# Two rows of a softmax to a partition: row-pair tiles, and template loads on another queue

## Chip, cores, metric

One Trainium2 chip, one of its cores, nothing else running. The metric is device microseconds (us) of one execution, lower is better; medians are over unprofiled and profiled executions of the same kernel. Profiles are single executions; their span is about 2 us shorter than the time. Profiled runs were fast (granted clock 1.0), and ratios use fast runs alone.

## The reference

A relative position bias is added to attention logits, then a softmax over the last axis:

```python
# logits (2, 8, 2112, 2112) float32, rel_bias (8, 33) float32
rel = clip(pos[:, None] - pos[None, :], -16, 16) + 16
logits = logits + rel_bias[:, rel]
e = exp(logits - logits.max(-1, keepdims=True))
return e / e.sum(-1, keepdims=True)
```

285.5 MB come in and 285.5 MB go out (2 x 8 x 2112 x 2112 x 4 bytes each). Outside a diagonal band 33 columns wide the bias is one constant per head on each side.

## The kernel before

The 33,792 rows of 2112 floats are cut into 264 tiles of 128 rows, one row to a partition. SyncE issues the load of a tile, VectorE (DVE) adds a band from a per-head template, ScalarE (ACT) takes exponentials left and right of the band's end with the constant as its bias and sums them, VectorE scales by the reciprocal, GpSimd (POOL) issues the store. SyncE also loads the templates.

```python
    io = ctx.enter_context(tc.tile_pool(name="io", bufs=20))
    ...
    def load_template(t, p0, np_, h):
        x = const.tile([P, BAND], FP32, tag="X", name="X", bufs=4)
        nc.sync.dma_start(out=x[p0 : p0 + np_], in_=bass.AP(... ap=[[1, np_], [1, BAND]]))
        nc.vector.tensor_copy(out=t[p0 : p0 + np_], in_=bass.AP(... [-1, BAND]))   # reversed
    ...
    for t in range(NT):                                  # 264 tiles
        rs = P * t
        ...
        L = io.tile([P, S], FP32, tag="L")
        nc.sync.dma_start(out=L, in_=logits_f[rs : rs + P, :])
        ...                                              # band add, exps with sums, per head segment
        nc.vector.reciprocal(out=tot, in_=tot)
        nc.vector.tensor_scalar_mul(out=L[:], in0=L[:], scalar1=tot[:])
        nc.gpsimd.dma_start(out=out_f[rs : rs + P, :], in_=L[:])
```

The softmax here doesn't subtract the row's maximum and nothing guards it: scores larger than these inputs give would overflow.

Of the kernel before, what the change touches and what calls it, by code (L numbers as in the profile page):

```python
# [1 line left out]

# [4 lines left out]

FP32 = mybir.dt.float32
EXP = mybir.ActivationFunctionType.Exp  # L10
ADD = mybir.AluOpType.add


@with_exitstack
def kernel(
    ctx: ExitStack,
    tc: tile.TileContext,
    logits: bass.AP,
    rel_bias: bass.AP,
    out: bass.AP,  # L20
):
    nc = tc.nc
    P = 128
    B, H, S, S2 = logits.shape
    assert S == S2
    MR = 16
    W = 2 * MR + 1
    BAND = P + 2 * MR
    EXT = P - 1
    ELEN = 2 * EXT + W  # L30

    logits_f = logits.flatten_outer_dims()
    out_f = out.flatten_outer_dims()
    NR = B * H * S
    assert NR % P == 0
    NT = NR // P

    const = ctx.enter_context(tc.tile_pool(name="const", bufs=1))
    dram = ctx.enter_context(tc.tile_pool(name="dram", bufs=1, space=bass.MemoryType.DRAM))

    rb8 = const.tile([H, W], FP32, tag="rb8")
    nc.sync.dma_start(out=rb8, in_=rel_bias)
    rbB = const.tile([P, H, W], FP32, tag="rbB")
    nc.sync.dma_start(
        out=rbB,
        in_=bass.AP(tensor=rel_bias.tensor, offset=rel_bias.offset, ap=[[0, P], [1, H * W]]),
    )

    e8 = const.tile([H, ELEN], FP32, tag="e8")
    nc.vector.tensor_copy(out=e8[:, 0:EXT], in_=rb8[:, 0:1].to_broadcast([H, EXT]))  # L50
    nc.vector.tensor_copy(out=e8[:, EXT : EXT + W], in_=rb8[:, :])  # L51
    nc.vector.tensor_scalar(  # L52
        out=e8[:, 0 : EXT + W],
        in0=e8[:, 0 : EXT + W],
        scalar1=rb8[:, W - 1 : W],
        scalar2=None,
        op0=mybir.AluOpType.subtract,
    )
    nc.vector.memset(e8[:, EXT + W :], 0.0)  # L59
    eD = dram.tile([H, ELEN], FP32, tag="eD")  # L60
    nc.sync.dma_start(out=eD, in_=e8)

    def load_template(t, p0, np_, h):
        x = const.tile([P, BAND], FP32, tag="X", name="X", bufs=4)
        nc.sync.dma_start(
            out=x[p0 : p0 + np_],
            in_=bass.AP(
                tensor=eD.tensor,
                offset=eD.offset + h * ELEN,
                ap=[[1, np_], [1, BAND]],  # L70
            ),
        )
        nc.vector.tensor_copy(  # L73
            out=t[p0 : p0 + np_],
            in_=bass.AP(
                tensor=x.tensor,
                offset=x.offset + p0 * list(x.ap[0])[0] + (BAND - 1),
                ap=[[list(x.ap[0])[0], np_], [-1, BAND]],
            ),
        )  # L80

    T = []
    for h in range(H):
        t = const.tile([P, BAND], FP32, tag=f"T{h}", name="T")
        load_template(t, 0, P, h)
        T.append(t)
    TP = []
    for k in range(H // 2):
        t = const.tile([P, BAND], FP32, tag=f"TP{k}", name="TP")
        load_template(t, 0, 64, 2 * k)  # L90
        load_template(t, 64, 64, 2 * k + 1)
        TP.append(t)
    io = ctx.enter_context(tc.tile_pool(name="io", bufs=20))
    small = ctx.enter_context(tc.tile_pool(name="small", bufs=16))

    def rb_at(h, k, p0, p1):
        return rbB[p0:p1, h, k : k + 1]

    for t in range(NT):
        rs = P * t  # L100
        f0 = rs // S
        f1 = (rs + P - 1) // S
        if f0 == f1:
            segs = [(0, P, f0, rs - f0 * S)]
        else:
            split = f1 * S - rs
            segs = [(0, split, f0, rs - f0 * S), (split, P, f1, 0)]

        L = io.tile([P, S], FP32, tag="L")
        nc.sync.dma_start(out=L, in_=logits_f[rs : rs + P, :])  # L110

        def seg_ab(p0, p1, i0):
            n = p1 - p0
            c0 = i0 - MR
            return c0, max(c0, 0), min(i0 + n + MR, S)

        max_slots = 1
        for (p0, p1, f, i0) in segs:
            _, _, b = seg_ab(p0, p1, i0)
            max_slots = max(max_slots, 1 + (b < S))  # L120

        s = None
        if max_slots == 2:
            s = small.tile([P, 2], FP32, tag="s", name="s")
        tot = small.tile([P, 1], FP32, tag="tot")

        for (p0, p1, f, i0) in segs:
            h = f % H
            n = p1 - p0
            c0, a, b = seg_ab(p0, p1, i0)  # L130
            nslots = 1 + (b < S)
            if len(segs) == 1:
                tmpl = T[h]
            else:
                tmpl = TP[(f0 % H) // 2]
            nc.vector.tensor_tensor(  # L136
                out=L[p0:p1, a:b],
                in0=L[p0:p1, a:b],
                in1=tmpl[p0 : p0 + n, a - c0 : b - c0],
                op=ADD,  # L140
            )
            acc0 = s[p0:p1, 0:1] if max_slots == 2 else tot[p0:p1, 0:1]
            nc.scalar.activation(  # L143
                out=L[p0:p1, 0:b],
                in_=L[p0:p1, 0:b],
                func=EXP,
                bias=rb_at(h, W - 1, p0, p1),
                accum_out=acc0,
            )
            if nslots == 2:  # L150
                nc.scalar.activation(  # L151
                    out=L[p0:p1, b:S],
                    in_=L[p0:p1, b:S],
                    func=EXP,
                    bias=rb_at(h, 0, p0, p1),
                    accum_out=s[p0:p1, 1:2],
                )
            elif max_slots == 2:
                nc.vector.memset(s[p0:p1, 1:2], 0.0)  # L159

        if max_slots == 2:
            nc.vector.tensor_tensor(out=tot, in0=s[:, 0:1], in1=s[:, 1:2], op=ADD)  # L162
        nc.vector.reciprocal(out=tot, in_=tot)  # L163

        nc.vector.tensor_scalar_mul(out=L[:], in0=L[:], scalar1=tot[:])  # L165

        nc.gpsimd.dma_start(out=out_f[rs : rs + P, :], in_=L[:])  # L167


# [1 line left out]
_INS = ['logits', 'rel_bias']  # L171
_OUTS = [((2, 8, 2112, 2112), 'float32')]


# [23 lines left out]
```

## Time and profile before

| | before |
|---|---|
| time, median | 1363.65 us (4 runs, 1362.85 to 1364.25) |
| span of the profile | 1361.6 us |
| DMA rate, steady part (100 to 1300 us) | 427.5 GB/s |
| bytes moved, all queues | 572.4 MB |
| span less bytes / steady rate | 1361.6 - 1339.1 = 22.5 us |
| ACT, DVE, POOL busy | 48%, 38%, 10% |

Rates to a tenth are summed from the packet records of the trace, between 100 and 1300 us; the views give whole GB/s. A packet is here one record of the profile: one contiguous run that one DMA engine moved. Besides the data there are records of 4 bytes, 9 ns long at the median, 16 to a DMA (8737 for the 547 DMAs of before); I take them for the signal that one of the 16 engines has done its part, and call them completions.

From the profile page of before: span, engine shares, then the span in 40 equal slices (tenths of the 16 DMA engines' busy time, and GB/s in each), the DMA queues with packets, MB and share of the 16 engines, the chain that ended last, and the issues with KB each and the median time to landing.

```profile
span 1361.6 us, 3994 instructions
DVE 518.4 (38%) x1084; ACT 657.6 (48%) x1057; POOL 140.6 (10%) x268
...
DMA  8999999999999999999999999999999999999996
GB/s 296 414 427 428 428 427 428 428 427 427 428 428 427 428 428 427 427 428 428 427 428 428 427 427 428 428 427 428 428 426 427 428 427 427 428 428 426 428 429 287
DMA packets 78030, 572.36 MB, mean 420 GB/s; under 512 B 8744, under 2 KB 10416, under 8 KB 10416
...
q1 hardware_dynamic: 39984, 286.62, 50.4%
q0 software_dynamic: 38016, 285.49, 49.7%
...
DMA 98%; issue 1%; DVE 0%; ACT 0%; SPq 0%; POOLq 0%; POOL 0%; ACTq 0%; DVEq 0%
...
L<-in_logits_dram SPq DMA_DIRECT2D x264, 1056.0 KB, 40.5
out_dram<-L POOLq DMA_DIRECT2D x264, 1056.0 KB, 15.2
```

No compute engine is busy more than half of the span (ACT, the most, 48%), while the two DMA queues together fill 100% of the 16 engines. The rate is flat at 426 to 429 GB/s and sags only in the first two slices and the last. So there are two things to gain: the rate itself, and the two ends. Of the packets, 2 x 33,792 are whole rows of 8448 B.

The beat of the steady part, from the timeline of before (start in us, duration, engine, line, operation):

```profile
305.82 0.53 POOL L167 DMA_DIRECT2D out_dram<-L  x1 [4.53 <-DVE L L165]
310.88 0.53 POOL L167 DMA_DIRECT2D out_dram<-L  x1 [4.52 <-DVE L L165]
315.94 0.53 POOL L167 DMA_DIRECT2D out_dram<-L  x1 [4.53 <-DVE L L165]
```

One tile every 5.06 us: 2,162,688 bytes in and out of it, so 427 GB/s.

What SyncE's queue waited for, from its waits (us in total, times, longest):

```profile
SPq L110 <- DMA L<-in_logits_dram: 1152.9, 252, 4.9
...
SPq L65 <- DMA X<-eD: 10.3, 7, 3.2
```

Each new load waits for an earlier load to land, not for a free buffer: with a landing time of 40.5 us and a beat of 5.06 us, eight loads are in flight at any time, and the 20 buffers are not what holds them. The second line is the start: on the same queue the template loads (L65) waited 10.3 us for their staging buffers, and the logits loads behind them waited too. By 22 us only five had been issued.

The two ends, from the stretch view of before (stretch, length, busy us of DVE, ACT, POOL with instruction counts, clock, DMA share, GB/s):

```profile
0.00:20.00 20.00, 6.22 (x20) 8.56 (x13) 1.41 (x6) 1.00 0.79 229
20.00:40.00 20.00, 7.91 (x21) 5.86 (x9) 1.55 (x3) 1.00 1.00 380
...
100.00:1300.00 1200.00, 460.57 (x952) 587.67 (x945) 125.92 (x237) 1.00 1.01 427
1337.00:1341.00 4.00, 0.95 (x3) 2.42 (x4) 0.53 (x1) 1.00 0.99 410
1341.00:1345.00 4.00, 1.71 (x4) 1.41 (x3) 0.00 (x0) 1.00 0.43 182
1345.00:1349.00 4.00, 2.08 (x5) 1.03 (x3) 1.06 (x2) 1.00 0.63 262
1349.00:1353.00 4.00, 1.48 (x2) 2.12 (x2) 0.03 (x1) 1.00 0.77 319
1353.00:1357.00 4.00, 0.00 (x0) 0.00 (x0) 0.50 (x1) 1.00 0.68 281
```

At the end the DMA engines run below their rate while ACT and DVE still work on the last tiles: nothing else is left to move.

### The profile page before, as it was taken

The numbers are of one execution on the slowest core, as the hardware profiler recorded it, in microseconds if no ns is written. First come the engines' busy times: TensorE is split into PE (matmuls) and PEld (weight loads), VectorE is DVE, ScalarE is ACT, GpSimd is POOL, SyncE is SP. The second block draws the span as 40 slices with busy tenths as digits, with TensorE's granted clock in tenths as the row PEclk, the third lists the DMA queues.
The fourth block names the chain that finished last, engine by engine and source line by source line (L and its number), as shares of the span: only waits on it lengthen the run. The fifth ranks groups of instructions, "written<-read, shape, count | busy, mean of one in ns | idle before, by whom it ended". The sixth has DMA issues, their size and how long they took to land.

```text
span 1361.6 us, 3994 instructions
## 1 busy us (share of the span) xinstructions
DVE 518.4 (38%) x1084; ACT 657.6 (48%) x1057; POOL 140.6 (10%) x268
## 2 busy tenths in 40 slices
DVE  3434343343334333333343333333433433333432
ACT  3454444544445444454444544445444454444543
POOL 0011011010101111011011010101101101101100
DMA  8999999999999999999999999999999999999996
GB/s 296 414 427 428 428 427 428 428 427 427 428 428 427 428 428 427 427 428 428 427 428 428 427 427 428 428 427 428 428 426 427 428 427 427 428 428 426 428 429 287
DMA packets 78030, 572.36 MB, mean 420 GB/s; under 512 B 8744, under 2 KB 10416, under 8 KB 10416
## 3 DMA queue, kind: packets, MB, share of 16 engines
q1 hardware_dynamic: 39984, 286.62, 50.4%
q0 software_dynamic: 38016, 285.49, 49.7%
q14 instruction: 30, 0.25, 0.0%
HBM read 286.59 MB, written 285.48 MB: 420 GB/s over the span
## 4 chain that ended last, share of the span: by engine, by line
DMA 98%; issue 1%; DVE 0%; ACT 0%; SPq 0%; POOLq 0%; POOL 0%; ACTq 0%; DVEq 0%
DMA L<-in_logits_dram 96%; DMA X<-eD 1%; DMA eD<-e 0%; ACT L L143 0%; SPq L110 0%; DMA rb<-in_rel_bias_dram 0%; DVE L L165 0%; DVE T L73 0%; POOLq L193 0%; DVE tot L162 0%; POOL out_dram L167 0%; ACT L L151 0%; DVE tot L163 0%; DVE L L136 0%; DVE e L52 0%
## 5 line engine op out<-in xcount | busy, mean ns | idle before, releaser
L151 ACT ACTIVATE L<-L,rbB 128x1968 f32<-128x1968 f32 (+31 forms) x256 | 297.1, 1160 | 654.0 <-DMA L<-in_logits_dram 651.0
L165 DVE TENSOR_SCALAR L<-L,tot 128x2112 f32<-128x2112 f32 x264 | 348.4, 1320 | 8.4
L143 ACT ACTIVATE L<-L,rbB 128x144 f32<-128x144 f32 (+33 forms) x272 | 333.2, 1225 | 30.5 <-DVE L L136 23.7
L167 POOL DMA_DIRECT2D out_dram<-L x264 | 140.4, 532 | 1212.7 <-DVE L L165 1050.2
L136 DVE TENSOR_TENSOR L<-L,T 128x160 f32<-128x160 f32 (+1 forms) x256 | 82.9, 324 | 350.3 <-DMA L<-in_logits_dram 348.9
L162 DVE TENSOR_TENSOR tot<-s 128x1 f32<-128x1 f32 x256 | 40.6, 159 | 422.9 <-ACT L L143 422.3
L163 DVE RECIPROCAL tot<-tot 128x1 f32<-128x1 f32 x264 | 43.2, 164 | 26.3 <-ACT L L143 17.7
L143 ACT ACTIVATION_READ_ACCUMULATOR L<-L,rbB 128x1 f32 (+1 forms) x272 | 50.7, 186 | 0.0
L151 ACT ACTIVATION_READ_ACCUMULATOR L<-L,rbB 128x1 f32 (+1 forms) x256 | 47.7, 186 | 0.0
L136 DVE TENSOR_TENSOR L<-L,TP 64x80 f32<-64x80 f32 x16 | 3.8, 236 | 7.2 <-DMA L<-in_logits_dram 6.9
L73 DVE COPY T<-X 128x160 f32<-128x160 f32 x8 | 1.7, 240 | 11.9 <-DMA X<-eD 11.9
L151 ACT ACT_TABLE_LOAD x1 | 1.3, 1283 | 9.1 <-DMA L<-in_logits_dram 9.1
L73 DVE COPY TP<-X 64x160 f32<-64x160 f32 x8 | 1.9, 238 | 5.2 <-DMA X<-eD 5.1
L50 DVE COPY e<-rb 8x127 f32<-8x127 f32 x1 | 0.2, 215 | 1.2 <-DMA rb<-in_rel_bias_dram 1.2
L59 DVE MEMSET e<- 8x127 f32 x1 | 0.2, 164 | 0.8 <-PEq L182 0.8
L159 DVE MEMSET s<- 64x1 f32 x8 | 0.5, 59 | 0.0
L52 DVE TENSOR_SCALAR e<-e,rb 8x160 f32<-8x160 f32 x1 | 0.3, 291 | 0.0
L51 DVE COPY e<-rb 8x33 f32<-8x33 f32 x1 | 0.2, 160 | 0.0
L182 POOL MEMSET const-float32-0.0<- 128x1 f32 x1 | 0.1, 98 | 0.2 <-issue 0.2
L182 POOL MEMSET const-bfloat16-1.0<- 128x1 bf16 x1 | 0.1, 102 | 0.0
L182 POOL MEMSET const-float32-1.0<- 128x1 f32 x1 | 0.1, 98 | 0.0
L182 POOL MEMSET const-uint8-127<- 128x1 uint8 x1 | 0.1, 98 | 0.0
## 6 DMA issues: line engine op xcount, KB each, us to landing
L<-in_logits_dram SPq DMA_DIRECT2D x264, 1056.0 KB, 40.5
out_dram<-L POOLq DMA_DIRECT2D x264, 1056.0 KB, 15.2
X<-eD SPq DMA_DIRECT2D x8, 80.0 KB, 4.4
X<-eD SPq DMA_DIRECT2D x8, 40.0 KB, 7.8
rbB<-in_rel_bias_dram SPq DMA_DIRECT2D x1, 132.0 KB, 5.3
rb<-in_rel_bias_dram SPq DMA_DIRECT2D x1, 1.0 KB
eD<-e SPq DMA_DIRECT2D x1, 9.0 KB
```

What stands on the lines that cost most here:

```text
L50: nc.vector.tensor_copy(out=e8[:, 0:EXT], in_=rb8[:, 0:1].to_broadcast([H, EXT]))
L52: nc.vector.tensor_scalar(out=e8[:, 0 : EXT + W], in0=e8[:, 0 : EXT + W], scalar1=rb8[:, W - 1 : W], scalar2=None, op0=mybir.AluOpType.sub ...
L73: nc.vector.tensor_copy(out=t[p0 : p0 + np_], in_=bass.AP(tensor=x.tensor, offset=x.offset + p0 * list(x.ap[0])[0] + (BAND - 1), ap=[[list ...
L136: nc.vector.tensor_tensor(out=L[p0:p1, a:b], in0=L[p0:p1, a:b], in1=tmpl[p0 : p0 + n, a - c0 : b - c0], op=ADD,)
L143: nc.scalar.activation(out=L[p0:p1, 0:b], in_=L[p0:p1, 0:b], func=EXP, bias=rb_at(h, W - 1, p0, p1), accum_out=acc0,)
L151: nc.scalar.activation(out=L[p0:p1, b:S], in_=L[p0:p1, b:S], func=EXP, bias=rb_at(h, 0, p0, p1), accum_out=s[p0:p1, 1:2],)
L159: nc.vector.memset(s[p0:p1, 1:2], 0.0)
L162: nc.vector.tensor_tensor(out=tot, in0=s[:, 0:1], in1=s[:, 1:2], op=ADD)
L163: nc.vector.reciprocal(out=tot, in_=tot)
L165: nc.vector.tensor_scalar_mul(out=L[:], in0=L[:], scalar1=tot[:])
L167: nc.gpsimd.dma_start(out=out_f[rs : rs + P, :], in_=L[:])
L182: nc = _bacc.Bacc("TRN2", target_bir_lowering=False, num_devices=1)
```

## The change

Its intent: make each DMA transfer longer and contiguous. A tile now takes 256 rows, and partition p holds rows 2p and 2p+1, which are neighbours in memory and in the partition: 16,896 contiguous bytes on both sides. Buffers become 9 of two rows. The last 256 rows stay two single tiles. Because a row in the band now moves by two columns per partition, templates are 287 columns wide instead of 160, a segment that starts inside a tile needs its own template, and the template loads move to POOL's queue with two staging buffers.

```diff
+    KB = 2
+    NTAIL = 2
...
     def load_template(...):
-        x = const.tile([P, BAND], FP32, tag="X", name="X", bufs=4)
-        nc.sync.dma_start(
+        x = const.tile([P, width], FP32, tag=f"X{width}", name="X", bufs=2)
+            nc.gpsimd.dma_start(                      # stride KB per partition
...
-    io = ctx.enter_context(tc.tile_pool(name="io", bufs=20))
+    io = ctx.enter_context(tc.tile_pool(name="io", bufs=9))
...
-        L = io.tile([P, S], FP32, tag="L")
-        nc.sync.dma_start(out=L, in_=logits_f[rs : rs + P, :])
+        L = io.tile([P, kb, S], FP32, tag=f"L{kb}", bufs=9 if kb == KB else 2)
+        nc.sync.dma_start(
+            out=L,
+            in_=logits_f[rs : rs + n, :].rearrange("(p j) c -> p j c", j=kb),
+        )
...                                                    # per j: band add, exps, scale
-        nc.gpsimd.dma_start(out=out_f[rs : rs + P, :], in_=L[:])
+        nc.gpsimd.dma_start(
+            out=out_f[rs : rs + n, :].rearrange("(p j) c -> p j c", j=kb),
+            in_=L[:],
+        )
```

More of the change, by code (lines that the diff above doesn't have):

```diff
@@ L27 @@
     W = 2 * MR + 1
-    BAND = P + 2 * MR
-    EXT = P - 1
+    KB = 2
+    NTAIL = 2
+    EXT = KB * (P - 1)
     ELEN = 2 * EXT + W
@@ L34 @@
     NR = B * H * S
-    assert NR % P == 0
-    NT = NR // P
+    assert NR % (KB * P) == 0
+    NBLK = NR // (KB * P) - (NTAIL + KB - 1) // KB
     const = ctx.enter_context(tc.tile_pool(name="const", bufs=1))
@@ L61 @@
     nc.sync.dma_start(out=eD, in_=e8)
-    def load_template(t, p0, np_, h):
-        x = const.tile([P, BAND], FP32, tag="X", name="X", bufs=4)
-        nc.sync.dma_start(
-            out=x[p0 : p0 + np_],
-            in_=bass.AP(
-                tensor=eD.tensor,
-                offset=eD.offset + h * ELEN,
-                ap=[[1, np_], [1, BAND]],
-            ),
-        )
-        nc.vector.tensor_copy(
-            out=t[p0 : p0 + np_],
-            in_=bass.AP(
-                tensor=x.tensor,
-                offset=x.offset + p0 * list(x.ap[0])[0] + (BAND - 1),
-                ap=[[list(x.ap[0])[0], np_], [-1, BAND]],
-            ),
-        )
@@ L82, with legal_split @@
-    T = []
-    for h in range(H):
-        t = const.tile([P, BAND], FP32, tag=f"T{h}", name="T")
-        load_template(t, 0, P, h)
-        T.append(t)
-    TP = []
-    for k in range(H // 2):
-        t = const.tile([P, BAND], FP32, tag=f"TP{k}", name="TP")
-        load_template(t, 0, 64, 2 * k)
-        load_template(t, 64, 64, 2 * k + 1)
-        TP.append(t)
-    io = ctx.enter_context(tc.tile_pool(name="io", bufs=20))
+    def legal_split(p0, p1):
+        return [(p0, min(64, p1)), (64, p1)] if 0 < p0 < 64 < p1 else [(p0, p1)]
@@ new lines, in load_template @@
+    def load_template(t, p0, np_, h, stride, width):
+        off0 = EXT + 2 * MR - (width - 1)
+        assert off0 >= 0 and off0 + stride * (np_ - 1) + width <= ELEN
+        x = const.tile([P, width], FP32, tag=f"X{width}", name="X", bufs=2)
+        xpitch = list(x.ap[0])[0]
+        for (pa, pb) in legal_split(p0, p0 + np_):
+            nc.gpsimd.dma_start(
+                out=x[pa:pb],
+                in_=bass.AP(
+                    tensor=eD.tensor,
+                    offset=eD.offset + h * ELEN + off0 + stride * (pa - p0),
+                    ap=[[stride, pb - pa], [1, width]],
+                ),
+            )
+            nc.vector.tensor_copy(
+                out=t[pa:pb],
+                in_=bass.AP(
+                    tensor=x.tensor,
+                    offset=x.offset + pa * xpitch + (width - 1),
+                    ap=[[xpitch, pb - pa], [-1, width]],
+                ),
+            )
@@ new lines @@
+    W2 = KB * (P - 1) + 2 * MR + 1
+    W1 = (P - 1) + 2 * MR + 1
+    tmpl_req = {}
+    groups = []
+    r = 0
+    while r < NR:
+        kb = KB if r < NBLK * KB * P else 1
+        n = kb * P
+        f0 = r // S
+        f1 = (r + n - 1) // S
+        if f0 == f1:
+            segs = [(0, P, f0, r - f0 * S)]
+        else:
+            sp = (f1 * S - r) // kb
+            assert sp * kb == f1 * S - r and 0 < sp < P
+            segs = [(0, sp, f0, r - f0 * S), (sp, P, f1, 0)]
+        out_segs = []
+        for (p0, p1, f, i0) in segs:
+            h = f % H
+            key = (p0, h, kb)
+            if key not in tmpl_req:
+                tmpl_req[key] = (p0, P - p0, h, kb, W2 if kb == KB else W1)
+            out_segs.append((p0, p1, f, i0, key))
+        groups.append((r, kb, out_segs))
+        r += n
@@ L94 @@
+    assert r == NR
+    TMPL = {}
+    for key, (p0, np_, h, stride, width) in sorted(tmpl_req.items()):
+        t = const.tile([P, width], FP32, tag=f"T{key}", name="T")
+        load_template(t, p0, np_, h, stride, width)
+        TMPL[key] = t
+    io = ctx.enter_context(tc.tile_pool(name="io", bufs=9))
     small = ctx.enter_context(tc.tile_pool(name="small", bufs=16))
@@ L97, in rb_at @@
         return rbB[p0:p1, h, k : k + 1]
-    for t in range(NT):
-        rs = P * t
-        f0 = rs // S
-        f1 = (rs + P - 1) // S
-        if f0 == f1:
-            segs = [(0, P, f0, rs - f0 * S)]
-        else:
-            split = f1 * S - rs
-            segs = [(0, split, f0, rs - f0 * S), (split, P, f1, 0)]
-        L = io.tile([P, S], FP32, tag="L")
-        nc.sync.dma_start(out=L, in_=logits_f[rs : rs + P, :])
-        def seg_ab(p0, p1, i0):
-            n = p1 - p0
-            c0 = i0 - MR
-            return c0, max(c0, 0), min(i0 + n + MR, S)
-        max_slots = 1
-        for (p0, p1, f, i0) in segs:
-            _, _, b = seg_ab(p0, p1, i0)
-            max_slots = max(max_slots, 1 + (b < S))
-        s = None
-        if max_slots == 2:
-            s = small.tile([P, 2], FP32, tag="s", name="s")
-        tot = small.tile([P, 1], FP32, tag="tot")
-        for (p0, p1, f, i0) in segs:
-            h = f % H
-            n = p1 - p0
-            c0, a, b = seg_ab(p0, p1, i0)
-            nslots = 1 + (b < S)
-            if len(segs) == 1:
-                tmpl = T[h]
-            else:
-                tmpl = TP[(f0 % H) // 2]
+    for (rs, kb, segs) in groups:
+        n = kb * P
+        L = io.tile([P, kb, S], FP32, tag=f"L{kb}", bufs=9 if kb == KB else 2)
+        nc.sync.dma_start(
+            out=L,
+            in_=logits_f[rs : rs + n, :].rearrange("(p j) c -> p j c", j=kb),
+        )
+        s = small.tile([P, kb, 2], FP32, tag="s")
+        tot = small.tile([P, kb], FP32, tag="tot")
+        maxslots = [1] * kb
+        info = []
+        for (p0, p1, f, i0, key) in segs:
+            np_ = p1 - p0
+            ww = kb * (np_ - 1) + 2 * MR + 1
+            pranges = legal_split(p0, p1)
+            for j in range(kb):
+                c0 = i0 + j - MR
+                a = max(c0, 0)
+                b = min(c0 + ww, S)
+                if b < S:
+                    maxslots[j] = 2
+                for (pp0, pp1) in pranges:
+                    info.append((pp0, pp1, f, i0, key, j, c0, a, b))
+        for (p0, p1, f, i0, key, j, c0, a, b) in info:
+            h = f % H
+            tmpl = TMPL[key]
@@ L136 @@
             nc.vector.tensor_tensor(
-                out=L[p0:p1, a:b],
-                in0=L[p0:p1, a:b],
-                in1=tmpl[p0 : p0 + n, a - c0 : b - c0],
+                out=L[p0:p1, j, a:b],
+                in0=L[p0:p1, j, a:b],
+                in1=tmpl[p0:p1, a - c0 : b - c0],
                 op=ADD,
             )
-            acc0 = s[p0:p1, 0:1] if max_slots == 2 else tot[p0:p1, 0:1]
+            nslots = 1 + (b < S)
+            acc0 = s[p0:p1, j, 0:1] if maxslots[j] == 2 else tot[p0:p1, j : j + 1]
@@ L143 @@
             nc.scalar.activation(
-                out=L[p0:p1, 0:b],
-                in_=L[p0:p1, 0:b],
+                out=L[p0:p1, j, 0:b],
+                in_=L[p0:p1, j, 0:b],
                 func=EXP,
@@ L151 @@
                 nc.scalar.activation(
-                    out=L[p0:p1, b:S],
-                    in_=L[p0:p1, b:S],
+                    out=L[p0:p1, j, b:S],
+                    in_=L[p0:p1, j, b:S],
                     func=EXP,
                     bias=rb_at(h, 0, p0, p1),
-                    accum_out=s[p0:p1, 1:2],
+                    accum_out=s[p0:p1, j, 1:2],
                 )
-            elif max_slots == 2:
-                nc.vector.memset(s[p0:p1, 1:2], 0.0)
-        if max_slots == 2:
-            nc.vector.tensor_tensor(out=tot, in0=s[:, 0:1], in1=s[:, 1:2], op=ADD)
-        nc.vector.reciprocal(out=tot, in_=tot)
-        nc.vector.tensor_scalar_mul(out=L[:], in0=L[:], scalar1=tot[:])
-        nc.gpsimd.dma_start(out=out_f[rs : rs + P, :], in_=L[:])
+            elif maxslots[j] == 2:
+                nc.vector.memset(s[p0:p1, j, 1:2], 0.0)
+        js = [j for j in range(kb) if maxslots[j] == 2]
+        if js:
+            j0, j1 = js[0], js[-1] + 1
+            nc.vector.tensor_tensor(
+                out=tot[:, j0:j1], in0=s[:, j0:j1, 0], in1=s[:, j0:j1, 1], op=ADD
+            )
+        nc.vector.reciprocal(out=tot[:, 0:kb], in_=tot[:, 0:kb])
+        for j in range(kb):
+            nc.vector.tensor_scalar_mul(
+                out=L[:, j, :], in0=L[:, j, :], scalar1=tot[:, j : j + 1]
+            )
+        nc.gpsimd.dma_start(
+            out=out_f[rs : rs + n, :].rearrange("(p j) c -> p j c", j=kb),
+            in_=L[:],
+        )
 _INS = ['logits', 'rel_bias']
```

## The prediction

> **What bounds it now.** The DMA engines, by their own rate. The 40-slice view shows DMA at 9 tenths in every slice between the first and the last, at 426 to 429 GB/s in nearly all. ACT is busy 48%, DVE 38%, POOL 10% of 1361.6 us; the chain of waits is 96% loads of L. In the timeline one 128-row tile repeats every 5.055 us: 2 x 1.0813 MB / 5.055 us = 428 GB/s. All 572.4 MB at 427.8 GB/s are 1338 us. The other 22 us are the two ends (stretch view): by 40 us only 12.2 MB had moved of 17.1 possible (11.5 us lost: SyncE's queue waits for template loads between logits loads), and after 1340 us 4.6 MB in 21.6 us (10.8 us lost).
>
> [...]
>
> **What the change does.**
> - Two consecutive rows go to one partition, so a row pair is contiguous (16,896 B) on both sides. If a pair becomes one packet, packets (78,030) fall to about 40,000[...]. If pairs stay two packets, only completions halve[...].
> - ACT does the same per-row exponentials. The add grows from 160 to 287 columns, estimated 0.33 to 0.47 us from its 80- and 160-column times, +35 us of DVE; some 260 small sums and reciprocals disappear, -40 us. POOL issues 133 stores for 264. All off the path.
> - Template loads leave SyncE's queue for POOL's, so DMA should fill from about 3 us (up to -6 us). Against it: 17 template loads, 1.8 MB for 0.96 (+2 us), two staging buffers, on one in-order queue with the stores. If stores queue behind all templates, the 9 double buffers (19.5 MB, 46 us of loads) fill and DMA idles. Estimated -4 to +20 us, centre -1.
> - Buffers: a pair tile has 9 x 10.1 = 91 us for load, work (about 9 us) and store (about 25 us): enough to keep the queue full. The last 256 rows stay single tiles, so the end costs the same within 3 us.
>
> Sum: 1363.65[...] - 1: **1354 us**, range **1342 to 1370**. Chances: faster by over 2% 0.02, within 2% 0.95, slower 0.03.
>
> **What would show it.** Right: packets near 40,000, 431 to 432 GB/s in the steady slices, 10.02 to 10.05 us per pair, chain still loads of L. The packet step is wrong if packets stay near 74,000, or halve while GB/s stays 428 (then the loss is not per packet). The start is wrong if the first slices move less than 296 and 414 GB/s, or POOL's stores begin after 50 us.
>
> **What would make it wrong.** Template loads blocking stores at the start; SyncE waiting for free buffers, so that DMA has gaps; coarser packets making loads and stores alternate worse[...].

The sum came to 1354 us: 1363.65, less some 8 for the step in packets, less 1 for the start and the template bytes.

## The result and the profile after

The changed kernel took 1346.0 us (median of 8 runs, 1345.81 to 1346.73), the kernel before 1363.33 us in the same rounds. The ratio is 0.9873, 95% interval 0.9864 to 0.9883, so 1.3% faster and inside the 2% that counts as the same. Ratios here and below are the mean time of one kernel's fast runs over that of the other's fast runs of the same rounds, so not quite the ratio of the medians quoted.

From the profile page of after, the lines that answer to those of before:

```profile
span 1344.2 us, 3115 instructions
DVE 495.9 (37%) x867; ACT 696.5 (52%) x1123; POOL 86.7 (6%) x154
...
DMA  9999999999999999999999999999999999999997
GB/s 371 413 417 433 428 433 433 429 432 431 430 433 429 431 433 428 433 431 430 432 431 430 433 429 431 434 429 432 432 430 432 429 432 433 428 433 431 430 432 326
DMA packets 39192, 573.02 MB, mean 426 GB/s; under 512 B 4568, under 2 KB 4712, under 8 KB 5120
...
another core or an unknown queue 43%; DMA 37%; ACT 4%; SPq 2%; DVE 1%; issue 1%; POOLq 0%; ACTq 0%; POOL 0%; DVEq 0%
...
L<-in_logits_dram SPq DMA_DIRECT2D x131, 2112.0 KB, 17.7
out_dram<-L POOLq DMA_DIRECT2D x131, 2112.0 KB, 63.7
```

Packets halved, 78,030 to 39,192: a pair did become one packet. The steady slices rose from 426 to 429 to 428 to 434 GB/s, and the first and last slices are fuller; the second is not (413 for 414), and the third is lower (417 for 427). The two landing times have changed places: loads now land after 17.7 us, stores after 63.7. (The chain of this profile is of little use: for 43% of it the profile could not name the releaser.) SyncE's queue shows the same turn in its waits: it now waits for stores to give buffers back.

```profile
SPq L135 <- DMA out_dram<-L: 1209.8, 122, 33.8
```

From the stretch view of after, the start, the steady part and the end:

```profile
0.00:20.00 20.00, 1.75 (x6) 5.63 (x7) 2.51 (x8) 1.00 0.86 335
20.00:40.00 20.00, 9.18 (x19) 8.53 (x15) 5.80 (x7) 1.00 1.01 425
60.00:80.00 20.00, 6.45 (x12) 4.32 (x8) 2.61 (x4) 1.00 1.00 390
100.00:1300.00 1200.00, 457.72 (x792) 655.03 (x1055) 68.01 (x124) 1.00 1.01 431
...
1328.00:1332.00 4.00, 0.00 (x0) 0.00 (x0) 0.00 (x0) 1.00 0.97 414
1332.00:1336.00 4.00, 0.00 (x0) 0.00 (x0) 0.00 (x0) 1.00 0.85 359
1336.00:1340.00 4.00, 0.00 (x0) 0.00 (x0) 0.00 (x0) 1.00 0.20 82
1340.00:1344.00 4.00, 0.00 (x0) 0.00 (x0) 0.00 (x0) 1.00 0.04 15
```

By 1317 us no engine computes any more (timeline); the stores that had piled up drain at full rate, then fade out over some 8 us.

The difference can be booked. "Lost" is time less bytes over the kernel's own steady rate, in the first 100 us and after 1300 us; rates and bytes are summed from the packet records:

| | before | after | difference |
|---|---|---|---|
| steady rate, GB/s | 427.47 | 431.18 | |
| bytes, MB | 572.42 | 573.07 | +1.5 us |
| bytes of before at that rate, us | 1339.1 | 1327.6 | -11.5 us |
| lost at the start, us | 11.6 | 7.4 | -4.2 us |
| lost at the end, us | 11.0 | 7.8 | -3.2 us |
| span, us | 1361.6 | 1344.2 | -17.4 us |

So two thirds are rate; the other third is the two ends, 7.4 us, less 1.5 us for added template bytes. The lost times come from one profile each and are good to about 0.1 us.

### The profile page after: what moved, and what is told of

The parts are those of the page before. It is cut to its first block, busy times and chain, and to the rows that moved or that the text cites. A ratio compares the mean times of both kernels' runs of the same rounds, so it can differ in the third digit from the quotient of the medians.

```text
span 1344.2 us, 3115 instructions
## 1 busy us (share of the span) xinstructions
DVE 495.9 (37%) x867; ACT 696.5 (52%) x1123; POOL 86.7 (6%) x154
## 2 busy tenths in 40 slices
DMA packets 39192, 573.02 MB, mean 426 GB/s; under 512 B 4568, under 2 KB 4712, under 8 KB 5120
## 4 chain that ended last, share of the span: by engine, by line
another core or an unknown queue 43%; DMA 37%; ACT 4%; SPq 2%; DVE 1%; issue 1%; POOLq 0%; ACTq 0%; POOL 0%; DVEq 0%
DMA L<-in_logits_dram 26%; DMA out_dram<-L 11%; ACT L L177 3%; SPq L135 2%; ACT L L169 1%; DVE L L196 1%; DVE L L161 0%; DVE tot L193 0%; DVE tot L190 0%; ACTq L177 0%; POOLq L229 0%; POOL out_dram L200 0%; POOLq L200 0%; DVEq L161 0%
## 5 line engine op out<-in xcount | busy, mean ns | idle before, releaser
L177 ACT ACTIVATE L<-L,rbB 128x1841 f32<-128x1841 f32 (+52 forms) x265 | 310.0, 1170 | 457.5 <-DMA L<-in_logits_dram 457.4
L169 ACT ACTIVATE L<-L,rbB 32x2112 f32<-32x2112 f32 (+56 forms) x296 | 369.7, 1249 | 149.0 <-DVE L L161 148.3
L196 DVE TENSOR_SCALAR L<-L,tot 128x2112 f32<-128x2112 f32 x264 | 336.7, 1317 | 4.6
L161 DVE TENSOR_TENSOR L<-L,T 128x287 f32<-128x287 f32 (+11 forms) x296 | 114.8, 425 | 410.3 <-DMA L<-in_logits_dram 409.2
L200 POOL DMA_DIRECT2D out_dram<-L x133 | 73.0, 549 | 1167.5 <-DVE L L196 982.1
L190 DVE TENSOR_TENSOR tot<-s 128x2 f32<-128x2 f32 x129 | 20.5, 159 | 330.4 <-ACT L L169 288.0
L169 ACT ACTIVATION_READ_ACCUMULATOR L<-L,rbB 128x1 f32 (+3 forms) x296 | 55.1, 186 | 0.0
L177 ACT ACTIVATION_READ_ACCUMULATOR L<-L,rbB 128x1 f32 (+2 forms) x265 | 49.3, 186 | 0.0
L193 DVE RECIPROCAL tot<-tot 128x2 f32<-128x2 f32 (+1 forms) x133 | 22.1, 166 | 17.0 <-ACT L L169 12.6
L75 POOL DMA_DIRECT2D X<-eD x17 | 13.5, 799 | 62.3 <-DVE T L83 36.2
## 6 DMA issues: line engine op xcount, KB each, us to landing
L<-in_logits_dram SPq DMA_DIRECT2D x131, 2112.0 KB, 17.7
out_dram<-L POOLq DMA_DIRECT2D x131, 2112.0 KB, 63.7
```

The costliest lines, as they stand in the source:

```text
L75: nc.gpsimd.dma_start(out=x[pa:pb], in_=bass.AP(tensor=eD.tensor, offset=eD.offset + h * ELEN + off0 + stride * (pa - p0), ap=[[stride, pb ...
L161: nc.vector.tensor_tensor(out=L[p0:p1, j, a:b], in0=L[p0:p1, j, a:b], in1=tmpl[p0:p1, a - c0 : b - c0], op=ADD,)
L169: nc.scalar.activation(out=L[p0:p1, j, 0:b], in_=L[p0:p1, j, 0:b], func=EXP, bias=rb_at(h, W - 1, p0, p1), accum_out=acc0,)
L177: nc.scalar.activation(out=L[p0:p1, j, b:S], in_=L[p0:p1, j, b:S], func=EXP, bias=rb_at(h, 0, p0, p1), accum_out=s[p0:p1, j, 1:2],)
L190: nc.vector.tensor_tensor(out=tot[:, j0:j1], in0=s[:, j0:j1, 0], in1=s[:, j0:j1, 1], op=ADD)
L193: nc.vector.reciprocal(out=tot[:, 0:kb], in_=tot[:, 0:kb])
```

## The experiments

Theory A: each packet costs an engine a fixed time, whatever its length, so fewer and longer packets raise the rate; the ends are a separate gain from the template move. Rival B: fewer DMAs (completions, issues) raise the rate. Rival C: only the ends matter. Five rounds each, beside the kernel before on the same chip.

### Pairs kept apart: two packets again

```diff
-        L = io.tile([P, kb, S], FP32, ...)
+        L = io.tile([P, kb, S + 8], FP32, ...)      # the two rows no longer touch in SBUF
-            out=L,                  /   in_=L[:]
+            out=L[:, :, 0:S],       /   in_=L[:, :, 0:S]
```

Expected:

> The change with each row pair padded apart in SBUF by 8 floats, so that a pair is two packets of 8448 B; as few DMAs, the same buffers and templates. Theory A (overhead per packet): packets back near 73,000, steady rate from about 431 to about 428 GB/s, time 1354 to 1356 us, the ends as in the kernel after. Rival B (fewer, larger DMAs and completions do it): steady rate stays at 431 GB/s, time within 2 us of the kernel after (1346). Rival C (the gain is only at the two ends): also 1346.

Measured: 1354.43 us, ratio to before 0.993 (0.9916 to 0.9943). From the profile page:

```profile
GB/s 362 412 420 428 428 428 428 428 428 429 428 428 428 427 428 428 428 428 428 428 428 428 428 428 429 428 428 427 428 428 429 428 428 428 428 427 428 428 428 341
DMA packets 72728, 573.02 MB, mean 424 GB/s; under 512 B 4568, under 2 KB 4712, under 8 KB 5120
```

The same DMAs, bytes, buffers and templates, only with 72,728 packets: the rate falls back to 428.05 GB/s and 8.4 us of time return. Of the step from 427.47 to 431.18, halving the DMAs gave 0.6 and merging the rows 3.1. Rivals B and C are out as the main cause, and A holds. The pad also shifts the second row's address in SBUF, but that is not what slows it: its packets take 319 ns at the median, like those of before.

### Rows cut in half: twice the packets of before

```diff
-        nc.sync.dma_start(out=L, in_=logits_f[rs : rs + P, :])
+        for c in (0, S // 2):
+            nc.sync.dma_start(out=L[:, c : c + S // 2], in_=logits_f[rs : rs + P, c : c + S // 2])
```

(and the store likewise, on the kernel before). Expected:

> The kernel before with each load and each store cut into two column halves, so packets of 4224 B. The steady periods of before, the padded pairs, after and three rows (5.060, 5.053, 5.016, 5.001 us per 128 rows) fit 4.6 ns per packet and 7 ns per completion on one engine. Theory A (a fixed cost per packet at any size) then adds 16 packets and 2 completions per tile: 5.060 + 0.087 = 5.147 us, 420 GB/s in the steady part, time 1383 to 1391 us. Rival (what helps is something that only sets in for packets larger than 8448 B, and below it the rate is flat): 1363 to 1369 us.

Measured: 1391.71 us, ratio 1.0202 (1.0188 to 1.0216). The steady rate is 419.7 GB/s, as foretold; the time is 1 us above the range: the end lost 13.5 us and not 11, and the rate dipped to 409 GB/s between 1260 and 1300 us, for which no cause was found.

```profile
GB/s 289 416 420 420 420 420 420 420 420 420 420 420 420 420 420 420 420 419 420 420 420 420 420 420 420 420 420 420 420 420 420 419 417 420 420 420 410 417 420 255
DMA packets 154075, 572.50 MB, mean 412 GB/s; under 512 B 17192, under 2 KB 18864, under 8 KB 154032
```

The cost per packet works below 8448 B as above it.

### Three rows to a partition

`KB = 3`, 6 buffers in place of 9, otherwise the changed kernel. Expected:

> The change with three rows to a partition (25,344 B packets, 6 buffers of them, so the same bytes of buffer; 3 single tiles at the end). Theory A: a fit of 5.059 us (1 row) and 5.020 us (2 rows) per 128 rows gives 5.007 for 3 rows, 432 GB/s in the steady part, about 27,000 packets; time 1341 to 1345 us. Rival B, if fewer DMAs count and not packets, gives the same; a rival in which coarse packets hurt gives 431 or less and more than 1346.

Measured: 1352.03 us, ratio 0.9916 (0.9903 to 0.993). The rate came as expected, 432.4 GB/s with 26,868 packets, but the time was 6 us slower than the changed kernel, not faster. The whole loss is at the end: 16.3 us lost there for 7.8. With three rows to a tile the last 384 rows are three single tiles, and there are two buffers for singles. From its timeline, the third single's load and what followed:

```profile
1318.37 0.53 POOL L200 DMA_DIRECT2D out_dram<-L  x1 [0.43 <-issue]
1330.79 0.33 SPq L135 DMA_DIRECT2D L<-in_logits_dram  x1
...
1336.23 2.05 ACT L169 ACTIVATE L<-L,rbB 128x2112 f32<-128x2112 f32 x1 [23.28 <-DVE L L161]
...
1340.22 0.53 POOL L200 DMA_DIRECT2D out_dram<-L  x1 [21.32 <-DVE L L196]
```

The last load went out at 1330.79 us, when the first single's store had landed; ACT stood idle for 23 us, until 1336.23. A tail meant to be short had become the longest part of the end. The remedy was tried next.

### The same without single tiles

`KB = 3`, `NTAIL = 0`, 6 buffers. Expected:

> Three rows to a partition as before, but no single tiles at the end: in the earlier run the third single tile's load had to wait for a store, as there are only two buffers for singles. Steady rate 432.4 GB/s as there; the end after 1300 us loses 7 to 9 us and not 16; time 1342 to 1346 us. If it stays at 1350 or more, the long end belongs to three rows themselves (a larger last store, more work after the last load).

Measured: 1343.43 us, ratio 0.9849 (0.9835 to 0.9862). The rate stayed at 432.5, the end lost 9.4 us. So the tail had been the main fault, not the three rows: 6.9 of the 8.5 us by which that end was longer than the changed kernel's are gone, 1.6 us remain.

And two rows with `NTAIL = 0`. Expected:

> The change with two rows throughout, no single tiles at the end. Theory (a pile of some 60 us of stores covers the work after the last load, so the last tile's size does not matter): time 1344 to 1347 us. Rival (single tiles make the end short): a pair needs about 5 us more of work and 2.5 us more of store after its load, so 1350 to 1354 us.

Measured: 1345.89 us, ratio 0.9868 (0.9854 to 0.9881), the end lost 7.7 us. The single tiles of the change buy nothing. What follows the last load is covered by stores that are still waiting their turn.

### Template loads, each way

On the kernel before, only the queue of the template loads changed (`nc.sync` to `nc.gpsimd`). Expected:

> The kernel before with one word changed: template loads issued by POOL and not by SyncE. Theory (the start is a separate gain): steady rate unchanged at 427 to 428 GB/s, more bytes moved by 40 us than the 12.2 MB of before, time 1356 to 1360 us. If stores are put behind the templates and pile up, the end gets shorter as well, and the time falls to 1355 or 1356. Rival (everything is the packets): 1363.

Measured: 1359.08 us, ratio 0.9966 (0.9953 to 0.9978). The rate is unchanged, 427.45. The start lost 6.6 us for 11.6, and the end 0.5 us more than before: together the 4.5 us gained. Stores did pile up (38.3 us to landing for 15.2), but the end, with 11.5 us lost for 11.0, did not get shorter. From its stretch view:

```profile
1341.00:1345.00 4.00, 0.00 (x0) 0.00 (x0) 0.00 (x0) 1.00 0.86 361
1345.00:1349.00 4.00, 0.00 (x0) 0.00 (x0) 0.00 (x0) 1.00 0.20 84
1349.00:1353.00 4.00, 0.00 (x0) 0.00 (x0) 0.00 (x0) 1.00 0.09 36
```

Compute is over by then, as a pile should have it, but the drain fades over 12 us in place of stopping at once.

On the changed kernel, the template loads put back on SyncE's queue. Expected:

> The change with the template loads put back on SyncE's queue. Theory (the ends gain 7 us by moving the templates, at the start by not holding up loads, at the end by a pile of stores that covers the last tile's work): steady rate stays 431 GB/s, first 60 us move less, loads land later and stores sooner than after (17.7 and 63.7 us), time 1350 to 1354 us. Rival (the move is worth nothing, fewer tiles made the ends shorter): 1346.

Measured: 1348.55 us (1346.39 to 1350.98), ratio 0.9888 (0.9874 to 0.9902). The rate stayed, 431.2. Landing times went as the theory said, to near balance:

```profile
L<-in_logits_dram SPq DMA_DIRECT2D x131, 2112.0 KB, 41.5
out_dram<-L POOLq DMA_DIRECT2D x131, 2112.0 KB, 40.1
...
SPq L75 <- DMA X<-eD: 49.1, 9, 12.1
```

The last line is from the waits of SyncE's queue: it stood 49.1 us for staging buffers.

The start lost 9.9 us, 2.5 more than in the changed kernel, but the end lost 6.6, no more than there. So in this profile the move of the templates is worth 2.5 us at the start (5.0 in the kernel before), and the median time is under the expected range. The part of the theory that gave the move the shorter end as well is not borne out. The spread of 4.6 us is wide, and the times alone would not settle a difference of 2.5. Only one execution was profiled, at 1347.25 us; what made two of the others 2.6 and 3.7 us longer is not known.

### Six buffers in place of nine

`bufs=6` on the changed kernel. Expected:

> The change with 6 pair buffers and not 9. Theory (buffers only carry the start, where stores wait behind templates; in the steady part the rest of them merely holds finished tiles in the store queue): steady rate unchanged at 431 GB/s, stores land in about 33 us and not 64, loads still in about 18; the first 100 us lose 8 to 15 us more than after (7.4), time 1352 to 1362 us. Rival (9 pairs are needed to keep the queues full): steady rate under 428 GB/s and a time above 1365.

Measured: 1345.62 us, ratio 0.9868 (0.9854 to 0.9881).

```profile
L<-in_logits_dram SPq DMA_DIRECT2D x131, 2112.0 KB, 18.3
out_dram<-L POOLq DMA_DIRECT2D x131, 2112.0 KB, 32.3
```

The steady half of the theory came to the microsecond: three tiles fewer, 31 us less in the store queue, the rate 431.2 as before. The other half was wrong: the start lost 7.2 us and not 15 or more. Buffers seven to nine carried nothing, not even the start; they only stood in the store queue.

### Late templates, and how far longer packets go

A segment that starts at partition p can read its head's ordinary template from column KB x p on, so 8 templates do for 17 loads, and each is loaded two tiles before its first use:

```diff
-                in1=tmpl[p0:p1, a - c0 : b - c0],
+                in1=tmpl[p0:p1, kb * t0 + a - c0 : kb * t0 + b - c0],   # t0: first partition of the segment
...
+    for g, (rs, kb, segs) in enumerate(groups):
+        for h, first in tmpl_req.items():
+            if max(0, first - 2) == g:
+                template_for(h)
```

With two rows (9 buffers, no singles), expected:

> Two rows to a partition, no single tiles, the 8 late templates: beside the two-row kernel without singles (1345.9) it shows what the templates alone are worth. Theory: steady rate unchanged at 431.2 GB/s, 1 MB fewer template bytes (2 us), start 1 to 3 us less lost: 1341 to 1343.5 us. Rival (templates cost nothing that counts): 1345 to 1346.

Measured: 1342.99 us, ratio 0.9846 (0.9833 to 0.986). The rate is nearly the same (430.95), 0.4 MB are saved and the start lost 5.0 us for 7.7. I had expected 1 MB: that mis-stated the bytes, the time holds. (This experiment and the next two ran in other rounds on another chip than the one compared with; the ratios, 0.9846 for 0.9868, give the same 3 us.) Loads landed in 16.6 us and stores in 64.8, as in the changed kernel.

With three rows (6 buffers, no singles), expected:

> A version meant to beat both: three rows to a partition, no single tiles, and only 8 templates (a segment that starts at partition p reads the head's one template shifted by 3p columns), each loaded two tiles before its first use and not all at the start. Theory (rate by packets, start by template traffic): steady rate 432.4 GB/s as with three rows before; bytes 573.5 to about 573; the first 100 us lose 4 to 5 us for 6.4; time 1339 to 1342 us against 1343.4 with the templates at the start. If the start does not gain, 1343.

Measured: 1340.90 us (1340.82 to 1340.96), ratio 0.9831 (0.9818 to 0.9845). It is the fastest of all, 5 us under the changed kernel by the medians: rate 432.5, start 4.6 us lost, end 9.4.

With six rows (3 buffers), expected:

> The same with six rows to a partition (50,688 B packets) and 3 buffers. The law of 4.6 ns per packet gives 4.988 us per 128 rows, 433.6 GB/s, 8 us less than two rows in the steady part, but templates are 3.3 MB (+4 us on 8 of two rows), and a tile's work (about 17 us) and transfers (15 us each way) are long for three buffers. Theory: the rate holds at 433 GB/s or a little over, the two ends lose 20 to 30 us in place of 15; time 1344 to 1356 us. If three buffers do not keep the queues full, the steady rate falls below 430 and the time is above 1360.

Measured: 1454.34 us, ratio 1.0672 (1.0647 to 1.0698), the last of its named outcomes. From the profile page and the waits of SyncE's queue:

```profile
DMA  9799999987999999996999999999599999999958
GB/s 389 298 384 372 440 424 411 435 338 306 429 403 424 397 426 425 401 432 290 392 431 409 419 422 427 426 402 440 253 416 431 378 419 427 426 422 408 418 254 380
```

```profile
SPq L137 <- DMA out_dram<-L: 1348.9, 41, 80.0
```

Loads and stores each take 34 us to land and a tile's six rows are worked on in between; with three tiles the queues run dry again and again, and the mean steady rate is 402.8 GB/s. Three big buffers did not do what six smaller ones of the same bytes did. That the number of tiles at different stages is what counts is argued from these waits; three buffers of fewer rows were not run.

### The law

Steady rates as the time for 128 rows (2,162,688 bytes over the rate), with what a DMA engine handles in that time on average (a sixteenth of all):

| kernel | packet, B | packets | completions | GB/s | us per 128 rows |
|---|---|---|---|---|---|
| half rows | 4224 | 32 | 4 | 419.68 | 5.153 |
| before | 8448 | 16 | 2 | 427.47 | 5.059 |
| pairs apart | 8448 | 16 | 1 | 428.05 | 5.052 |
| after | 16,896 | 8 | 1 | 431.18 | 5.016 |
| three rows, no singles | 25,344 | 5.33 | 0.67 | 432.49 | 5.001 |

From pairs apart to after, 8 packets are worth 37 ns: 4.6 ns each. From before to pairs apart, one completion is worth 7 ns (that step also changed the buffers and the queue of the templates, but neither moved the rate when changed alone: 431.2 and 427.45). With these, half rows should stand 16 x 4.6 + 2 x 7 = 87 ns above before; measured 94, or 88 without the dip, from 100 to 1000 us (420.2 GB/s). Three rows should stand 2.67 x 4.6 + 0.33 x 7 = 15 ns under after; measured 15. Only the half rows were foretold by this law before they ran.

The packet records show the same from within. The median packet takes 164, 319, 629, 940 and 1872 ns for 4224, 8448, 16,896, 25,344 and 50,688 B: 310 or 311 ns for each further 8448 B, that is 27.2 GB/s, plus 8 to 9 ns whatever the length. About half of those 9 ns shows in the rate. The other half goes into records that overlap: in before, 16 x 319 + 2 x 9 = 5122 ns of records stand in a beat of 5059, some 4 ns a packet (the DMA share is 1.013, and 1.006 after, above 1). Why they overlap was not tested.

## Why the prediction was right

- **The bound.** DMA rate with compute hidden: right. Every experiment that changed the packets changed the rate (419.7 GB/s with half rows, 428.05 with pairs apart, 432.5 with three rows, for 427.47 before and 431.18 after), and the compute work did not matter. ACT's busy time rose by 39 us; the prediction missed that, and it cost nothing. There are 24 more row segments to work on (296 for 272): 16 because more tiles of two rows contain a border between heads (12 for 8), 8 because segments that start at partition 32 are cut in two. The estimate for the wider add was right, 454 ns where 0.47 us stood.
- **The ceiling.** Nothing here shows where the engines' rate comes from. What the traces do show is how near the rate came to that of the packets: a packet of 8448 B takes 319 ns and one of 16,896 B 629 ns, so each further 8448 B take 310 ns or a little more, and 16 engines at that pace would move some 435 GB/s (an estimate from these records). The best steady rate seen was 432.5.
- **The packet step.** "If a pair becomes one packet, packets (78,030) fall to about 40,000." Measured: 39,192 packets, 5.016 us per 128 rows for 5.059, -11.5 us at equal bytes. The sum of the prediction took some 8 us for this step, between its estimates for a pair that merges and for one that does not, as it was not known which would happen; that hedge is 3.5 us of the 8 by which the centre of 1354 missed. Measured are 4.6 ns a packet and 7 ns a completion. The expected sign for it in the profile, 431 to 432 GB/s, was met (431.2). The cause is shown: keeping the pair apart takes the rate back to 428.05.
- **The completions.** "If pairs stay two packets, only completions halve." Pairs apart stand at 428.05 GB/s against 427.47, 1.8 us over the whole.
- **The start.** "Estimated -4 to +20 us, centre -1." Measured -4.2 us lost at the start and +1.5 us for template bytes, net -2.7: 1.7 us better than the centre. Nine logits loads of two rows were issued by 11.7 us, where before had issued five of one row by 22 us. The prediction's own sign for the start, first slices of at least 296 and 414 GB/s, was met by the first slice (371) and just missed by the second (413). The feared blocking of stores was mild: the first store went out at 30.0 us, and one stretch (60 to 80 us) sank to 390 GB/s. The move alone is worth 5.0 us in the kernel before and 2.5 in the changed one. Who issues the templates did not change the rate (427.45 GB/s for 427.47). What held back the start of before was the order of SyncE's queue: its timeline shows template and logits loads issued in turn (X at 12.14 us, L at 15.29, X at 17.96, L at 21.93), and its waits 10.3 us for staging buffers, with the logits loads behind them.
- **The end.** "The end costs the same within 3 us." Measured 3.2 us less, a gain that the prediction had no reason for. In before the last tile's work and store lay bare; after, it lies under waiting stores. That the pile covers the work is shown: going without singles changed nothing. That the pile alone makes the end shorter is not: the kernel before with its stores piled up lost 11.5 us at the end, in a drain that fades over 12 us. The short end goes with tiles of two rows: all six such kernels lost 6.6 to 7.8 us there, with the rows padded apart or not and with stores landing in 32 or in 64 us, where one row lost 11.0 and 11.5 and three rows without singles 9.4. Why stays open. In the fading drain of the changed kernel, 5, 3 and 1 us before the last packet ended, 4, 3 and 2 packets were under way where 16 are at full rate, each of the usual length (319 ns). So a few engines still had work, at their usual speed; why they had more left is not shown, as the trace as read here does not tell the 16 engines apart.
- **The buffers.** "Load, work (about 9 us) and store (about 25 us): enough to keep the queue full." The conclusion was right and the picture wrong: stores took 63.7 us to land, loads 17.7. In before, eight loads in flight was the limit; after, the buffers are, and most of them stood in the store queue. With the templates back on SyncE's queue the same buffers split 41.5 and 40.1. It is not that templates held up the stores at the start: the first nine stores of the changed kernel landed in 16 to 23 us, the pile grew between 120 and 200 us, and it is as large (64.8 us) with late templates, of which one is loaded at the start. What settles the split stays open. None of it touched the rate, and six buffers do as well as nine. The expected sign "chain still loads of L" did not hold: 26% of the chain are loads, 11% stores, and 43% the profile could not name.

Booked against the sum of the prediction, -9 us: rate -11.5 where -8 stood, start with bytes -2.7 where -1 stood, end -3.2 where 0 stood; -17.4 us. The time fell inside the range by a mechanism that was right in its main part; the three terms all missed to the same side.

## What to carry to other kernels

When a profile shows the DMA engines full at a flat rate, look at the packet size as well as the bytes: laying out neighbouring rows in one partition so that a transfer is contiguous on both sides pays a fixed cost per packet less often, here 4.6 ns of 319, which with fewer completions is worth 0.9% for the first doubling and 0.3% for the next step, and a pad of 32 bytes gives most of it back (0.7 of the 0.9%). Then book the two ends apart from the rate, since they were a third of the gain here. The start was won by other means: nothing that waits in the queue of the bulk loads (5.0 us in the kernel before, 2.5 in the changed one), templates loaded late and few (2.7 us with two rows). The end got shorter too, for a reason not found. Count tiles as well as bytes when buffers get bigger: six tiles of three rows kept the queues full (432.5 GB/s), three tiles of six rows, in the same bytes, did not (402.8).
